# A decoder layer in split float32: one weight sum of each seven-product step made by an accumulating transfer, and seven such steps of eight in the late chunks

## The chip, the cores and the metric

The kernel runs on one core of a Trainium2 chip. The metric is the device time of one execution in microseconds (us), the median of the runs; lower is better. The engines that matter here are TensorE (PE in the profile), VectorE (DVE), ScalarE (ACT), GpSimd (POOL) and SyncE (SP), which issues nearly all the loads. The transfers themselves run on 16 DMA engines that all the queues share.

## The reference

One layer over 256 tokens of 2048 features. Two gated feed-forward blocks stand around a mixer; the change touches only the first product of the feed-forward blocks.

```python
D_MODEL = 2048; SEQ = 256; D_FF = 5632

def swiglu(h, w_in, w_out):
    gu = h @ w_in                                  # (256, 2048) @ (2048, 11264)
    gate, up = gu[..., :D_FF], gu[..., D_FF:]
    return (jax.nn.silu(gate) * up) @ w_out        # (256, 5632) @ (5632, 2048)

h = h + 0.5 * swiglu(rmsnorm(h, ffn1_norm), ffn1_w_in, ffn1_w_out)
...                                                # pooling mixer and gated linear attention
h = h + 0.5 * swiglu(rmsnorm(h, ffn2_norm), ffn2_w_in, ffn2_w_out)
out = rmsnorm(h, final_norm)
```

All inputs and outputs are float32.

## The kernel before

**Split products.** A float32 number is held as a high part (a cast to the type fp32r, made by ACT, `L155`) and a low part (the number minus its high part, made by DVE, `L156`). A product of two such blocks is three matmuls: high by high, high by low, low by high (`three`, matmuls at `L191`). Every weight block that PE uses has to be split first, since weights are read from memory once each.

**Steps.** Weights come in steps of four blocks of 128 x 512, two loads of 512 KB each (`load`, `L135`): two blocks of input rows by two blocks of output columns, B11, B12, B21 and B22. Against the two token tiles (128 tokens each) such a step is a 2 by 2 block product. It is done in one of two ways. An *S step* makes all eight block products: 24 matmuls, and DVE makes four low parts (2048 columns). A *W step* is one step of a Strassen-Winograd scheme: seven block products, 21 matmuls, for which DVE also makes four differences of weight blocks (`less`, `L179`) and then the low parts of seven blocks in all. The activations' sums S1 to S4 that the scheme needs are made once for each pair of input blocks that may be used so (`W_PAIRS`, `s_make`). `KINDS` says which steps of a chunk are W and which are S.

**Chunks.** The 5632 hidden columns are 11 chunks of 512. `first_product(c)` multiplies chunk c of gate and up in eight steps, then gates and transposes the result. `second_product` multiplies finished chunks by the output weights, in S steps only; from chunk 2 on a first product of eight steps alternates with a second product over two chunks, four S steps. So a period in the middle of a feed-forward block has 12 steps. The first feed-forward block has names with f (`ps_fi`, `pw_fi`, `ps_fo`), the second with z.

**The combine.** The W steps of a chunk add four of their products up in the two tiles `pw_..._0` and `pw_..._1` of the accumulator memory. When the last W step is through, `combine` reads them: ACT copies one half of `pw_0` (`L297`), DVE makes four sums (`L298` to `L301`; the first reads the other half of `pw_0`, and `L301` is the last to read `pw_1`). The next second product accumulates in the space of the same two tiles: its token tile 0 takes that of `pw_0`, tile 1 that of `pw_1`. Then `L483` adds the sums to the chunk's own accumulators, `L490` and `L492` gate them, and `L505` splits the transposed result.

**Buffers.** Raw weights land in four slots of four blocks (three named `ring_raw`, one more `fring_raw` or `zring_raw`, taken in rotation). Split blocks go to a ring of 22 block places (16 named `ring_hi`, `ring_lo`, 6 more `fring_...` or `zring_...`); a block's place is free once PE has used it. A run of blocks that meets the end of either part of the ring is split in two by `parts_of`.

**Order.** Every engine works its queue in order. The order of each queue is fixed at build time by a scheduler that models how long the instructions take; the program's text gives only the dependences. SP issues a load as soon as the blocks of the slot that it overwrites have been read for the last time.

**POOL** issues the accumulating stores of half sums (`hd<-half`, `L537`: 512 KB added to a tensor in memory), two after each second product but the last ones, and does little else.

Of the kernel before, what the change touches and what calls it, by code (L numbers as in the profile page):

```python
# [33 lines left out]
ALU = mybir.AluOpType  # L34
PSUM = bass.MemoryType.PSUM

P = 128
# [5 lines left out]
CW = 512  # L43
# [15 lines left out]

W_PAIRS = (1, 3, 4, 6, 2, 5)  # L60
CHUNKS = ("WWWWWWSS",) * 8
KINDS = {
# [11 lines left out]
MORE_RAW = 1  # L74
MORE_RING = 6
WIDE = True
# [6 lines left out]
def layer(ctx: ExitStack, tc: tile.TileContext, io):  # L83
    nc = tc.nc
# [82 lines left out]
    def s_step(src, parts=1, runs=WIDE):  # L167

        w = load(src, parts=max(parts, 2)).rearrange("p (b c) -> p b c", c=CW)
        b = parts_of(w, SINGLES if parts == 4 else PAIRS if parts == 2 or not WIDE else ALL)  # L170
        return lambda k, n: b[n if k == 0 else 3 - n]

    def w_step(src):

        w = load(src).rearrange("p (b c) -> p b c", c=CW)
        f = dict(zip(("B11", "B22", "B21"), parts_of(w, (slice(0, 1), slice(2, 4)))))

        def less(out, x, y):
            nc.vector.tensor_tensor(out=out, in0=x, in1=y, op=ALU.subtract)  # L179


        less(w[:, 0:2, :], w[:, 1:2, :].broadcast_to([P, 2, CW]), w[:, 0:4:2, :])
        less(w[:, 2, :], w[:, 2, :], w[:, 0, :])
        less(w[:, 3, :], w[:, 3, :], w[:, 2, :])
        f.update(zip(("T1", "T3", "T2", "T4"), parts_of(w, PAIRS)))
        return f

    def three(ps, a, b, start, stop, **kw):

        for i, (x, y) in enumerate(((a[0], b[0]), (a[0], b[1]), (a[1], b[0]))):  # L190
            nc.tensor.matmul(ps, x, y, start=start and i == 0, stop=stop and i == 2, **kw)  # L191

    class Group:
# [66 lines left out]
        def w(self, a, s, b):  # L260

            if self.one is None:
# [6 lines left out]
                first = True  # L269
# [8 lines left out]
            three(p16[:, 0, :], a(0, 0), b["B11"], first, last)  # L278
            three(p75[:, 1, :], s["S1"], b["T1"], first, last)
            three(p75[:, 0, :], s["S3"], b["T3"], first, last)  # L280
# [7 lines left out]
        def combine(self):  # L288
# [6 lines left out]
            c, d = self.add  # L295
            u2 = d[:, 1, :]
            nc.scalar.copy(out=c[:, 0, :], in_=p16[:, 0, :])  # L297
            nc.vector.tensor_tensor(out=u2, in0=p16[:, 1, :], in1=c[:, 0, :], op=ALU.add)  # L298
            nc.vector.tensor_tensor(out=c[:, 1, :], in0=p75[:, 1, :], in1=u2, op=ALU.add)
            nc.vector.tensor_tensor(out=d[:, 0, :], in0=p75[:, 0, :], in1=u2, op=ALU.add)  # L300
            nc.vector.tensor_tensor(out=d[:, 1, :], in0=p75[:, 1, :], in1=d[:, 0, :], op=ALU.add)  # L301

# [831 lines left out]
```

## Time and profile before

| | |
|---|---|
| median of three runs | 1702.04 us (1701.92 to 1702.26) |
| span of the profiled execution | 1702.4 us, so 0.36 us above the median |
| PE, PEld, DVE, ACT, POOL busy | 1689.7, 1403.1, 1411.5, 999.3, 62.9 us |
| transfers | 365.30 MB, 215 GB/s over the span |
| a period of first and second product, first feed-forward block | 62.14 us, DVE busy in 59.10 us of it |

A matmul of 512 columns is listed with about 390 ns, but matmuls overlap: they start 0.227 us apart where PE has its operands. The same holds on DVE, where a listed duration is some 0.09 us longer than the distance of starts. What an instruction costs its engine is read from the distance of starts.

### The profile page before, as it was taken

To read this page: it belongs to the slowest core of one execution; us is meant where nothing else is said; L and a number is where in the kernel's file an instruction comes from. 1 tells how busy PE (TensorE), PEld (TensorE's weight loads), DVE (VectorE), ACT (ScalarE), POOL (GpSimd) and SP (SyncE) were. 2 spreads that over 40 slices of the span, in tenths; PEclk is the share of its full clock that TensorE was granted. 3 is DMA by queue.
4 is the path that set the end of the run, shared out by engine and by line. 5 is a ranking of instruction groups with operands and counts; after the bars stand their busy time and mean duration, and the time that the engine had idled before them with its cause. 6 is when DMAs were issued, how large, how long until landed. Compare 5 with 4: busy or idle time off the path is not lost.

```text
span 1702.4 us, 20984 instructions
## 1 busy us (share of the span) xinstructions
PE 1689.7 (99%) x7705; PEld 1403.1 (82%) x7705; DVE 1411.5 (83%) x1565; ACT 999.3 (59%) x1272; POOL 62.9 (4%) x70
## 2 busy tenths in 40 slices
PE   9999999999999999999999999999999999999997
PEld 7888888888888888888988888888888888888886
DVE  8779999999999996645564677999999999998974
ACT  7655666665666664563454554666656656566553
POOL 0000000000000000000000000000000000000012
PEclk9999999999999999999999999999999999999999
DMA  9856856857767776554665764676666667677781
GB/s 355 338 142 229 259 156 229 269 165 221 259 178 221 246 240 215 185 182 139 197 214 169 228 203 155 196 249 195 214 244 208 203 235 227 192 245 218 215 298 50
DMA packets 105241, 365.30 MB, mean 215 GB/s; under 512 B 11809, under 2 KB 15009, under 8 KB 105138
## 3 DMA queue, kind: packets, MB, share of 16 engines
q1 hardware_dynamic: 97026, 335.63, 58.1%
q0 software_dynamic: 7392, 27.27, 8.1%
q8 instruction: 60, 0.98, 0.2%
q10 hardware_dynamic: 720, 1.07, 0.2%
q14 instruction: 43, 0.35, 0.1%
HBM read 338.75 MB, written 25.17 MB: 214 GB/s over the span
## 4 chain that ended last, share of the span: by engine, by line
PE 91%; DVE 5%; DMA 2%; issue 1%; ACT 1%; SPq 0%; POOL 0%; POOLq 0%; ACTq 0%; DVEq 0%
PE ps_fi L191 17%; PE ps_zi L191 14%; PE ps_fo L191 14%; PE ps_zo L191 12%; PE pw_fi L191 8%; PE pw_zi L191 7%; PE ps_h L191 5%; PE ps_mp L191 3%; PE ps_mv L191 3%; DVE ring_lo L156 2%; PE ps_mg L191 2%; PE ps_mq L191 1%; DMA ring_raw<-in_ffn_w_out 1%; PE ps_w_mk L191 1%; DVE ring_raw L179 1%
## 5 line engine op out<-in xcount | busy, mean ns | idle before, releaser
L155 ACT CAST ring_hi<-ring_raw 128x1024 fp32r<-128x1024 f32 (+3 forms) x544 | 501.4, 942 | 381.6 <-DMA ring_raw<-in_ffn_w_in 79.8
L156 DVE TENSOR_TENSOR ring_lo<-ring_raw,ring_hi 128x1024 fp32r<-128x1024 f32 (+6 forms) x463 | 573.8, 1250 | 182.5 <-ACT ring_hi L155 181.4
L179 DVE TENSOR_TENSOR ring_raw<-ring_raw 128x512 f32<-128x512 f32 (+1 forms) x243 | 207.4, 862 | 0.3
L155 ACT CAST zring_hi<-ring_raw 128x1024 fp32r<-128x1024 f32 (+1 forms) x113 | 99.6, 887 | 54.5 <-DMA ring_raw<-in_ffn_w_out 11.8
L191 PE MATMUL ps_fi<-ring_lo,xT_hi 128*128 128x512 f32 x324 | 126.5, 390 | 0.5 <-DVE ring_lo L156 0.4
L191 PE MATMUL ps_fi<-ring_hi,xT_lo 128*128 128x512 f32 x324 | 125.8, 389 | 0.0
L191 PE MATMUL ps_fi<-ring_hi,xT_hi 128*128 128x512 f32 x324 | 124.2, 390 | 1.2 <-ACT ring_hi L155 1.2
L156 DVE TENSOR_TENSOR zring_lo<-ring_raw,zring_hi 128x1024 fp32r<-128x1024 f32 (+3 forms) x101 | 112.2, 1117 | 11.9 <-ACT zring_hi L155 11.8
L155 ACT CAST ring_hi<-zring_raw 128x1024 fp32r<-128x1024 f32 (+1 forms) x85 | 84.2, 991 | 48.0 <-PE ps_zi L191 22.8
L191 PE MATMUL ps_zi<-ring_lo,h_hi 128*128 128x512 f32 x288 | 112.1, 389 | 0.0
L191 PE MATMUL ps_zi<-ring_hi,h_lo 128*128 128x512 f32 x288 | 112.1, 390 | 0.0
L191 PE MATMUL ps_zi<-ring_hi,h_hi 128*128 128x512 f32 x288 | 111.3, 390 | 0.0
L156 DVE TENSOR_TENSOR ring_lo<-zring_raw,ring_hi 128x1024 fp32r<-128x1024 f32 (+2 forms) x65 | 94.2, 1451 | 7.4 <-ACT ring_hi L155 7.3
L191 PE MATMUL ps_fo<-ring_lo,fhi 128*128 128x512 f32 x240 | 93.9, 391 | 0.0
L191 PE MATMUL ps_fo<-ring_hi,flo 128*128 128x512 f32 x240 | 93.8, 391 | 0.0
L191 PE MATMUL ps_fo<-ring_hi,fhi 128*128 128x512 f32 x240 | 93.4, 391 | 0.0
L191 PE MATMUL pw_zi<-ring_hi,s_z 128*128 128x512 f32 x262 | 92.5, 389 | 0.0
L191 PE MATMUL ps_zo<-ring_lo,zhi 128*128 128x512 f32 x234 | 91.5, 391 | 0.0
L191 PE MATMUL ps_zo<-ring_hi,zlo 128*128 128x512 f32 x234 | 91.4, 391 | 0.0
L191 PE MATMUL ps_zo<-ring_hi,zhi 128*128 128x512 f32 x234 | 90.7, 390 | 0.0
L191 PE MATMUL pw_fi<-ring_hi,s_f 128*128 128x512 f32 x226 | 78.7, 389 | 0.0
L155 ACT CAST ring_hi<-fring_raw 128x512 fp32r<-128x512 f32 (+1 forms) x69 | 56.9, 832 | 33.6 <-DVE fring_raw L179 9.8
(324 smaller groups left out, 3730.5 us busy)
## 6 DMA issues: line engine op xcount, KB each, us to landing
ring_raw<-in_ffn_w_in SPq DMA_DIRECT2D x262, 512.0 KB, 5.6
ring_raw<-in_ffn_w_out SPq DMA_DIRECT2D x136, 512.0 KB, 5.2
fring_raw<-in_ffn_w_in SPq DMA_DIRECT2D x44, 512.0 KB, 5.5
zring_raw<-in_ffn_w_in SPq DMA_DIRECT2D x44, 512.0 KB, 4.3
ring_raw<-in_w_out_mix SPq DMA_DIRECT2D x32, 512.0 KB, 4.3
fring_raw<-in_ffn_w_out SPq DMA_DIRECT2D x20, 512.0 KB, 6.0
zring_raw<-in_ffn_w_out SPq DMA_DIRECT2D x20, 512.0 KB, 6.0
hd<-half_f POOLq DMA_DIRECT2D x18, 512.0 KB, 8.1
```

What stands on the lines that cost most here:

```text
L155: nc.scalar.copy(out=hi[:, j:k, :], in_=src[:, i + j : i + k, :])
L156: nc.vector.tensor_tensor(out=lo, in0=src[:, i : i + n, :], in1=hi.bitcast(F32), op=ALU.subtract)
L179: nc.vector.tensor_tensor(out=out, in0=x, in1=y, op=ALU.subtract)
L191: nc.tensor.matmul(ps, x, y, start=start and i == 0, stop=stop and i == 2, **kw)
```

## The change

Block order and signs of the W step are chosen anew, so that one of the four sums that it needs, Q1 = B12 + B11, can be made where B12 lies: after the load, a transfer issued by POOL reads B11 once more from memory (256 KB) and adds it to the block. DVE then makes three differences in two instructions instead of four in three: first one block, Q1 - B22, then in one instruction of two blocks B11 and B21 minus that. The low parts are made in two instructions, of three blocks (B11, B22, B21) and of four (Q1, T3, T2, T4), where they were four instructions of one and two blocks. In the combine two sums become differences. The late chunks (3 to 10) of both feed-forward blocks have seven W steps and one S step instead of six and two; for this the activation sums of one more pair are made, and the ring has 21 places instead of 22.

```diff
-W_PAIRS = (1, 3, 4, 6, 2, 5)
-CHUNKS = ("WWWWWWSS",) * 8
+W_PAIRS = (1, 3, 4, 6, 2, 5, 0)
+CHUNKS = ("WWWWWWWS",) * 8
...
-MORE_RING = 6
+MORE_RING = 5
...
     def w_step(src):
         w = load(src).rearrange("p (b c) -> p b c", c=CW)
-        f = dict(zip(("B11", "B22", "B21"), parts_of(w, (slice(0, 1), slice(2, 4)))))
+        nc.gpsimd.dma_start(out=w[:, 0, :], in_=src[:, CW : 2 * CW], accum_op=ALU.add)
+        f = dict(zip(("B11", "B22", "B21"), parts_of(w, (slice(1, 4),))))
...
-        less(w[:, 0:2, :], w[:, 1:2, :].broadcast_to([P, 2, CW]), w[:, 0:4:2, :])
-        less(w[:, 2, :], w[:, 2, :], w[:, 0, :])
-        less(w[:, 3, :], w[:, 3, :], w[:, 2, :])
-        f.update(zip(("T1", "T3", "T2", "T4"), parts_of(w, PAIRS)))
+        less(w[:, 2, :], w[:, 0, :], w[:, 2, :])
+        less(w[:, 1:4:2, :], w[:, 1:4:2, :], w[:, 2:3, :].broadcast_to([P, 2, CW]))
+        f.update(zip(("Q1", "T3", "T2", "T4"), parts_of(w, ALL)))
...
-            three(p75[:, 1, :], s["S1"], b["T1"], first, last)
+            three(p75[:, 1, :], s["S1"], b["Q1"], first, last)
...
-            nc.vector.tensor_tensor(out=c[:, 1, :], in0=p75[:, 1, :], in1=u2, op=ALU.add)
+            nc.vector.tensor_tensor(out=c[:, 1, :], in0=p75[:, 1, :], in1=u2, op=ALU.subtract)
...
-            nc.vector.tensor_tensor(out=d[:, 1, :], in0=p75[:, 1, :], in1=d[:, 0, :], op=ALU.add)
+            nc.vector.tensor_tensor(out=d[:, 1, :], in0=p75[:, 1, :], in1=d[:, 0, :], op=ALU.subtract)
```

After the change the lines from `w_step` on have numbers lower by one (the combine is `L296` to `L300`). PE has 48 matmuls fewer and DVE 226 instructions fewer; POOL issues 126 transfers more.

DVE in the middle of the W steps of chunk 7, first feed-forward block, before: `L156` rows are low parts, `L179` rows differences.

```order
L156 TENSOR_TENSOR fring_lo<-fring_raw,fring_hi 128x512
L156 TENSOR_TENSOR ring_lo<-ring_raw,ring_hi 128x1024
L156 TENSOR_TENSOR fring_lo<-fring_raw,fring_hi 128x1024
L179 TENSOR_TENSOR ring_raw<-ring_raw 128x512
L179 TENSOR_TENSOR fring_raw<-fring_raw 128x1024
L156 TENSOR_TENSOR ring_lo<-ring_raw,ring_hi 128x1024
L179 TENSOR_TENSOR ring_raw<-ring_raw 128x512
L156 TENSOR_TENSOR ring_lo<-ring_raw,ring_hi 128x2048
```

The same place now, with the semaphores waited on (`DMAHW` are loads from SP, `DMASW` transfers from POOL):

```order
L156 TENSOR_TENSOR ring_lo<-ring_raw,ring_hi 128x1536 [waits DMAHW2_49,DMAHW1_49,Activation_49]
L180 TENSOR_TENSOR ring_raw<-ring_raw 128x512 [waits DMASW1_49,DVE_49]
L156 TENSOR_TENSOR ring_lo<-fring_raw,ring_hi 128x2048 [waits Activation_49]
L180 TENSOR_TENSOR ring_raw<-ring_raw 128x2x512 [waits DVE_49]
L156 TENSOR_TENSOR ring_lo<-ring_raw,ring_hi 128x1536 [waits DMAHW4_49,DMAHW3_49,Activation_49]
```

A W step is now a row of 1536, one of 512, one of 2 x 512 and one of 2048 columns (with further cuts at the ring's ends), and the row of 512 is where DVE waits for the accumulating transfer; between it and the row of 2 x 512 of the same step stands the last low part of the step before.

PE at the end of the W steps of chunk 6, second feed-forward block, before: the last products into `pw_zi6_0`, then rows of the chunk's own accumulator. The last W product and an S step follow, 27 starts from the last row of `pw_zi6_0` to the first of the second product, `ps_zo0_4_0`.

```order
L191 MATMUL ps_zi6_0_9516<-ring_hi_74,h2_lo3_6517 128x512
L191 MATMUL pw_zi6_0_9531<-ring_lo_75,s_z2_7271 128x512 [waits DVE_49]
L191 MATMUL pw_zi6_0_9531<-ring_hi_74,s_z2_7271 128x512
L191 MATMUL ps_zi6_1_9517<-ring_lo_75,h2_hi2_6512 128x512
L191 MATMUL ps_zi6_1_9517<-ring_hi_74,h2_lo2_6516 128x512
```

The same place now:

```order
L190 MATMUL pw_zi6_1_9389<-ring_hi_74,s_z3_7174 128x512
L190 MATMUL pw_zi6_0_9388<-ring_lo_75,s_z3_7174 128x512
L190 MATMUL pw_zi6_0_9388<-ring_hi_74,s_z3_7174 128x512
L190 MATMUL ps_zi6_1_9375<-ring_lo_75,h2_hi0_6414 128x512
L190 MATMUL ps_zi6_1_9375<-ring_hi_74,h2_lo0_6418 128x512
```

From the last row of `pw_zi6_0` to the first of `ps_zo0_4_0` there are now 15 starts; half of the one S step that is left stands ahead of the last W products. So it is in 14 of the 19 chunks that have W steps; in the other five it is 20 to 38. Before it was 27 to 45 in all.

POOL in the first feed-forward block now; before, its queue held only the `hd<-half` rows there:

```order
L176 DMA ring_raw<-in_ffn_w_in 128x512 [waits DMAHW3_49,DMASW0_49,DVE_49]
L176 DMA ring_raw<-in_ffn_w_in 128x512 [waits DMAHW5_49,DMASW5_49,DVE_49]
L536 DMA hd<-half_f_2128 128x1024 [waits DMASW2_49,Activation_49]
L536 DMA hd<-half_f_2131 128x1024 [waits Activation_49]
L176 DMA fring_raw<-in_ffn_w_in 128x512 [waits DMAHW7_49,DMASW6_49,DVE_49]
L176 DMA ring_raw<-in_ffn_w_in 128x512 [waits DMAHW1_49,DMASW7_49,DVE_49]
```

The accumulating transfers of the W steps (`L176`) and the half sums (`L536`) share POOL's one queue in order: here the last two of a chunk's seven stand behind the half sums of the second product that came before the chunk.

More of the change, by code (lines that the diff above doesn't have):

```diff
@@ L1082, in steps @@
         b = b.transpose(3, 0, 2, 1, 4, 5)
-        b = np.stack([b[:, :, :, 0, 0], b[:, :, :, 0, 1], b[:, :, :, 1, 1], b[:, :, :, 1, 0]], 3)
+        b = np.stack([b[:, :, :, 0, 1], b[:, :, :, 0, 0], b[:, :, :, 1, 1], b[:, :, :, 1, 0]], 3)
         return b.reshape(b.shape[0], b.shape[1], P, 4 * CW)
```

2 lines of the change are left out of this document (1 added, 1 removed).

## The prediction

> **What bounds the kernel now.** I read the page first, for the span and the busy engines.
>
> ```profile
> span 1702.4 us, 20984 instructions
> ...
> PE 1689.7 (99%) x7705; PEld 1403.1 (82%) x7705; DVE 1411.5 (83%) x1565; ACT 999.3 (59%) x1272; POOL 62.9 (4%) x70
> ...
> DVE  8779999999999996645564677999999999998974
> ...
> DMA  9856856857767776554665764676666667677781
> ```
>
> PE is busy for 99% of the span, but DVE is at 9 tenths or more through both feed-forward blocks, where the change acts. So the next views are the windows (one period of 12 steps, then the first chunk of the second block) and PE's waits.
>
> ```profile
> core 0: us, PE busy (x) PEld busy (x) DVE busy (x) ACT busy (x) POOL busy (x), PEclk, DMA share, GB/s
> ...
> 334.25:396.39 62.14, 62.14 (x280) 51.46 (x279) 59.10 (x63) 39.20 (x47) 1.73 (x2) 1.00 0.70 217
> ...
> 1001.16:1087.35 86.19, 86.19 (x389) 71.42 (x389) 71.64 (x103) 48.10 (x66) 2.76 (x2) 1.00 0.52 174
> ```
>
> ```profile
> PE idle L575 <- DVE zeros L570: 1.2, 1, 1.2
> PE ps_fi L191 <- ACT ring_hi L155: 1.2, 2, 0.8
> PE ps_fi L191 <- DVE ring_lo L156: 0.4, 2, 0.2
> ```
>
> PE waits 2.8 us in the whole execution. DVE has 62.14 - 59.10 = 3.0 us to spare in a period, and PE never pays for it. So PE bounds and DVE follows closely: a matmul less is time less, until DVE or a transfer comes too late.
>
> What a matmul costs is read from the chain, since the busy list counts overlapped ends:
>
> ```profile
> 272.11 10.88 PE ps_fo L191 x48
> ```
>
> 10.88 / 48 = 0.2267 us. A W step of 21 is then 4.76 us on PE, an S step of 24 is 5.44 us.
>
> DVE's costs are read from the distance of starts in its timeline, at the end of chunk 6:
>
> ```profile
> 380.01 1.22 DVE L156 TENSOR_TENSOR ring_lo<-ring_raw,ring_hi 128x1024 fp32r<-128x1024 f32 x1
> 381.15 0.69 DVE L179 TENSOR_TENSOR fring_raw<-fring_raw 128x512 f32<-128x512 f32 x1
> 381.75 0.69 DVE L156 TENSOR_TENSOR fring_lo<-fring_raw,fring_hi 128x512 fp32r<-128x512 f32 x1
> 382.35 2.29 DVE L156 TENSOR_TENSOR ring_lo<-ring_raw,ring_hi 128x2048 fp32r<-128x2048 f32 x1
> 384.56 0.69 DVE L156 TENSOR_TENSOR ring_lo<-fring_raw,ring_hi 128x512 fp32r<-128x512 f32 x1
> 386.68 2.29 DVE L156 TENSOR_TENSOR fring_lo<-ring_raw,fring_hi 128x2048 fp32r<-128x2048 f32 x1 [1.44 <-ACT fring_hi L155]
> 388.89 2.29 DVE L156 TENSOR_TENSOR ring_lo<-ring_raw,ring_hi 128x2048 fp32r<-128x2048 f32 x1
> 391.09 0.69 DVE L298 TENSOR_TENSOR add_fi<-pw_fi,add_fi 128x512 f32<-128x512 f32 x1
> ...
> 393.49 1.75 DVE L156 TENSOR_TENSOR ring_lo<-fring_raw,ring_hi 128x1536 fp32r<-128x1536 f32 x1
> 395.15 0.69 DVE L156 TENSOR_TENSOR fring_lo<-fring_raw,fring_hi 128x512 fp32r<-128x512 f32 x1
> 395.76 1.23 DVE L483 TENSOR_TENSOR ps_fi<-ps_fi,add_fi 128x1024 f32<-128x1024 f32 x1
> 396.89 0.68 DVE L301 TENSOR_TENSOR add_fi<-pw_fi,add_fi 128x512 f32<-128x512 f32 x1
> ```
>
> 512 columns take 0.60 us, 1024 1.14, 1536 1.66, 2048 2.21.
>
> **The change, part by part.** *PE.* Two blocks times eight chunks lose one S step for a W step: 16 x 3 = 48 matmuls, the very number of the row above, 10.88 us. All of it lies on the path.
>
> *DVE.* A W step now costs 0.60 + 1.14 for the first low parts, 1.14 + 2 x 0.60 for the differences, 2 x 1.14 for the last low parts: 6.36 us. Then it costs 1.66 + 0.60 + 1.14 + 2.21 = 5.61 us. The rest of a period is four sums (2.40), two `L483` (2.28) and four rows of 512 (2.40): 7.1 us. Before: 6 x 6.36 + 6 x 2.21 + 7.1 = 58.5, beside the 59.10 listed. After: 7 x 5.61 + 5 x 2.21 + 7.1 = 57.4 in a period of 62.14 - 0.68 = 61.46. DVE's spare time grows from 3.0 to about 4.1 us, so its sum doesn't bound. Nor do the steps lag more: in the W run DVE loses 6 x (6.36 - 4.76) = 9.6 us on PE before, 7 x 0.85 = 6.0 after. ACT casts the same columns in a W step and 1536 more for each S step turned into one, beside 22 us of idle time in the period. The activation sums of the seventh pair (some 2 us of DVE in each block) fall in the first chunk, where DVE idles 14 us of 86.19 while PE is full. The ring's lost place is one block of 21, three matmuls or 0.7 us of lead, less than the 3.6 us by which the W run's lag shrinks. These four I cost at nothing.
>
> *The accumulating transfer: its issue and load on the queues.* Rows of the half sums and of the queues:
>
> ```profile
> L537 POOL DMA_DIRECT2D hd<-half_f x18: 853/862/1006, 107.7 to 607.5; - x18
> ...
> DMA to landing us min/median/max: 5.5/8.1/11.3
> ```
>
> ```profile
> q1 hardware_dynamic: 97026, 335.63, 58.1%
> q0 software_dynamic: 7392, 27.27, 8.1%
> ...
> ring_raw<-in_ffn_w_in SPq DMA_DIRECT2D x262, 512.0 KB, 5.6
> ...
> out<-zh SPq DMA_DIRECT2D x4, 256.0 KB, 2.9
> ```
>
> 126 issues of 0.86 us are 108 us of POOL, which is busy 4%. A packet of q1 takes 0.581 x 1702.4 x 16 / 97026 = 0.163 us, one of q0, 4 KB for nearly all, 0.298. The new packets are 2 KB, 128 to a step: between 0.149 (half the bytes) and 0.298 each, so 1.2 to 2.4 us of the 16 engines in a W step, beside 256 x 0.163 / 16 = 2.6 for its load. I take the lower end, since load packets too cost by their bytes: 3.8 us, under PE's 4.76. The period's DMA share goes from 0.70 to (43.5 + 8.3) / 61.46 = 0.84.
>
> *Its latency.* No row shows 256 KB added to on-chip memory. The nearest is the row above, 512 KB added in memory: 5.5 to 11.3 us to landing. Half the bytes under the same loads end near its lower end; I take 5.5, and the range keeps 2.9 (the nearest transfer of 256 KB, the output store) and 11.3. Where is it late? SP loads a slot as soon as DVE is done with it, and within the W run 11 to 18 us of other DVE rows stand between that and the difference that needs the sum. The tight place is the first W step of a chunk:
>
> ```profile
> 273.33 0.62 ACT L155 CAST ring_hi<-ring_raw 128x512 fp32r<-128x512 f32 x1 [4.24 <-DMA ring_raw<-in_ffn_w_in]
> 278.62 1.22 DVE L179 TENSOR_TENSOR ring_raw<-ring_raw 128x1024 f32<-128x1024 f32 x1
> ```
>
> ACT waits for that load until 273.33, and DVE's first difference starts 5.3 us later, filled with other work. A transfer of 5.5 us ends 0.2 us after this; DVE's additional 1.1 us of spare time covers that: nothing. If it lands at x us, PE loses about x - 5.3 - 1.1 in each chunk. What waits behind it on DVE is the whole queue, low parts of the next steps included; on POOL the half sums, which nothing needs for tens of us.
>
> *The combine's cover.* Between the last W product into `pw_0` and the second product that takes its place PE has 15 starts now in 14 chunks, 3.40 us, where 27 (6.12 us) to 45 stood. In that time ACT must copy and DVE make the first sum. Before, at the place of the DVE rows above and at one in the second block:
>
> ```profile
> 387.39 0.39 PE L191 MATMUL pw_fi<-fring_hi,s_f 128*128 128x512 f32 x1
> 388.45 0.58 ACT L297 COPY add_fi<-pw_fi 128x512 f32<-128x512 f32 x1
> 396.23 0.39 PE L191 MATMUL ps_fo<-ring_hi,fhi 128*128 128x512 f32 x1
> 1443.70 0.45 PE pw_zi L191 x2
> 1446.63 0.68 DVE L298 TENSOR_TENSOR add_zi<-pw_zi,add_zi 128x512 f32<-128x512 f32 x1
> ```
>
> The sum is done 391.09 + 0.69 - 387.39 = 4.4 us after the last product, and 3.4 to 3.6 in the second block, with wide low parts ahead of it in DVE's queue and 8.8 us of cover at the first of the two places. With 3.40 us, PE would wait 1.0 and 0.1 us if DVE kept its place. The new order puts less ahead of the sum (on average 3.2 us of rows behind the last low part of the W run, 4.5 before), which takes most of it away; the wait that is left is scatter. The bounds are 0 and 14 x 1.0; I take 0.2 us a chunk, 3 us in all, near the lower end, since a row of 4.4 less 1.3 is under 3.40. The other reads of `pw` have 9.5 us or more.
>
> *The sum.* 1702.4 - 10.9 + 3 = 1694.5 for the profiled execution; this stands 0.36 above the median of the runs, so 1694.2.
>
> **Two rules of the Trainium skill.** The issue row says 853 to 1006 ns while DVE was over 90% busy. The Trainium skill's SBUF — State Buffer (SBUF: two separate sides) warns that a transfer issued from GpSimd gets no descriptors while DVE holds the shared port in a two-port mode, and says that `tensor_tensor`, the only kind in these rows, has no such mode; the trace agrees so far, as no issue took 0.2 us above the others. As a rival: an issue held up by one DVE row of 2.29 us lands at 5.5 + 2.3 = 7.8, and PE loses 1.4 us in 16 chunks, 22 less 10.9, so 1713. The landing row is 5.5 to 11.3 us for 512 KB. The Trainium skill's DMA: Bandwidth & Descriptors (Anatomy of one DMA — SWDGE (gpsimd) path) gives 2.0 us plus the bytes at 436 GB/s: estimates by that page are 3.2 us for 512 KB, which the trace does not show, and 2.6 us for 256 KB, by which the first W step would have 2.7 us to spare and the sum would be the same.
>
> **The rivals.** (1) *The transfer lands late at the first W step of a chunk.* It decides from a landing of 5.3 + 1.1 + 0.68 = 7.1 us: from there PE loses more than it saves. For it: the half sums' median is 8.1 us, and ACT already waits there. Against: half the bytes. At 8.1 us PE loses 1.7 us in 16 chunks: 1702.0 - 10.9 + 27 = 1718. (2) *The short combine eats the gain.* If DVE keeps the place of the first-block row, 14 x 1.0 us is lost, with the five other chunks unhurt: 1702.0 - 10.9 + 14 = 1705; with half of that 1698. For it: the 4.4 us. Against: the 3.4 to 3.6. (3) *DMA engines become the bound of the W run.* At 0.298 us for a 2 KB packet a W step needs 2.6 + 2.4 = 5.0 us, over PE's 4.76, and the half sums' 512 packets (9.5 us) come in the same run: 7 x 5.0 + 9.5 = 44.5 us of transfers while PE needs 33.3. Three steps of lead in the ring (14.3 us) cover the 11.2 between them only if the ring is full at the start. A loss of 1 to 2 us a chunk gives 1707 to 1723. (4) *Everything new is hidden.* 1702.0 - 10.9 = 1691.1. PE has 2.8 us of waits in all, so not much less than this can come.
>
> **How the numbers follow.** The forecast with its neighbours, 1692.5 to 1697: 0.42. Rival 4, to 1692.5: 0.18. Rival 2, 1697 to 1706: 0.17, of which a third under 1698.6. Rival 1: 0.13. Rival 3: 0.07. The held-up issue: 0.03. A measurement of this kernel tells 0.2%, 3.4 us, from no change. Faster by more: 0.42 + 0.18 + 0.05 = 0.65. Within it, 1698.6 to 1705.4: 0.11 of rival 2 and 0.02 of the lower ends of rivals 1 and 3: 0.13. Slower: 0.22. The range goes from 1690.5 to 1709, which leaves out the upper parts of rivals 1 and 3, 0.16 or so, and little below. The forecast's own range is 1691 to 1698.
>
> **What the profile would show.** 1: the second product's first step starts 61.5 us after the one before, where it was 62.14. 2: DVE rows of a W step in four, 1.66, 0.60, 1.14, 2.21 apart, some 57 to 58 us busy in a period. 3: the accumulating transfers' landing at a median near 5.5 us, and DVE's waits (`L180`, or `L156` at the ring's end) for transfers small. 4: PE's waits for the first sum of the combine at or below 3 us in total. The prediction is wrong if the landing is over 7 us, if PE waits for `L297` by a us or more in a chunk, or if loads take clearly over their present 5.6 us.

## The result, and the profile after

The changed kernel takes 1787.13 us (median of five runs, 1784.43 to 1791.99) against 1702.04 (1701.49 to 1703.94) for the kernel before in the same comparison: a ratio of 1.0497, 95% interval 1.0484 to 1.051. It is 5% slower, 85 us, and far outside the predicted range. The profiled execution took 1785.36 us, with a span of 1783.6. (Of `plain`, among the experiments, one of two runs was in the chip's slower state and is left out.)

The page after, in the order of the lines shown of before (span, busy engines, the queues in packets, MB and share of 16 engines), and from the list of transfers the rows of loads and of the new accumulating ones (the number at the end is the median from issue to landing):

```profile
PE 1716.4 (96%) x7657; PEld 1404.6 (79%) x7657; DVE 1395.2 (78%) x1303; ACT 1011.5 (57%) x1276; POOL 175.8 (10%) x196
...
q1 hardware_dynamic: 97026, 335.63, 55.3%
q0 software_dynamic: 25536, 60.30, 18.9%
...
ring_raw<-in_ffn_w_in SPq DMA_DIRECT2D x262, 512.0 KB, 6.2
...
ring_raw<-in_ffn_w_in POOLq DMA_DIRECT2D x97, 256.0 KB, 5.0
fring_raw<-in_ffn_w_in SPq DMA_DIRECT2D x44, 512.0 KB, 7.7
```

PE has its 48 matmuls less (7705 to 7657), and DVE has less work too (1411.5 to 1395.2 us). By share PE, DVE and ACT are all less busy than before; only POOL, which issues the new transfers, does more (4% to 10%). PE's idle time, span less busy, goes from 12.7 to 67.2 us. So the time went into waiting. PE's waits, where before had three rows of 2.8 us together (columns: total us, times, longest us; the line numbers after the change are one lower, `L297` to `L300` are the sums of the combine, `L190` the matmuls):

```profile
PE pw_fi L190 <- DVE ring_lo L156: 12.7, 9, 2.7
PE pw_zi L190 <- DVE ring_lo L156: 7.9, 7, 2.0
PE ps_zo L190 <- DVE add_zi L297: 6.3, 3, 2.9
PE pw_fi L190 <- ACT ring_hi L155: 5.7, 7, 1.6
PE pw_zi L190 <- ACT ring_hi L155: 5.6, 7, 1.8
PE ps_fo L190 <- DVE add_fi L297: 4.6, 2, 2.4
PE ps_zo L190 <- DVE ring_lo L156: 3.5, 2, 2.7
```

Over all rows PE waits 41.9 us for split blocks (1.6 before), 13.2 us for the combine (0 before) and 1.2 us at the start. The second loss is the clock:

```profile
core 0: 1783.6 us, clock 0.984
```

It was 0.998. A mean clock of 0.984 over 1783.6 us is 28.5 us of full speed not granted, 3.4 before: up to 25 us. The spans then compare as -10.9 (matmuls) + 53.5 (waits) + 25 (clock) = 67.6 of the 81.2 us by which the two profiled executions differ (the medians differ by 85.1). The other 13.6 I can't assign row by row; some 8 of them are the way a wait is counted, from the modelled end of the matmul ahead, 0.39 us after its start, though starts come 0.23 apart (49 waits x 0.16).

Where it happens: the windows of one period in the first block, from a second product's start to the next, and slices of 4 us at the end of the W run (columns as in the prediction: length, then PE, PEld, DVE, ACT and POOL busy, PEclk, DMA share, GB/s):

```profile
481.21:553.20 71.99, 66.20 (x277) 52.28 (x276) 60.89 (x49) 40.81 (x48) 9.26 (x11) 0.95 0.85 243
...
536.00:540.00 4.00, 3.90 (x17) 2.88 (x16) 4.00 (x3) 1.42 (x2) 0.00 (x0) 1.00 0.73 222
540.00:544.00 4.00, 1.86 (x6) 0.67 (x4) 3.83 (x3) 3.37 (x4) 0.00 (x0) 1.00 0.92 280
544.00:548.00 4.00, 2.19 (x5) 1.81 (x6) 2.36 (x2) 0.19 (x1) 0.86 (x1) 0.54 0.96 343
548.00:552.00 4.00, 4.00 (x12) 3.10 (x12) 2.08 (x2) 2.67 (x4) 0.86 (x1) 0.60 1.03 338
552.00:556.00 4.00, 4.00 (x19) 3.30 (x19) 3.66 (x5) 3.00 (x3) 0.00 (x0) 1.00 1.06 270
```

The period takes 71.99 us, where 62.14 stood (the eight periods of the block have a mean of 66.8). DVE is busy 60.89 of it, so it has 11 us to spare, and PE still waits: in the slices from 540 to 548 us PE runs 11 matmuls where some 35 fit. Then the column PEclk falls to 0.54 and 0.60. In the timeline these are the last matmuls of the W run (start, us, row, what ended the wait):

```profile
542.23 0.51 PE L190 MATMUL pw_fi<-ring_hi,s_f 128*128 128x512 f32 x1 [1.61 <-ACT ring_hi L155]
543.18 0.50 PE L190 MATMUL pw_fi<-ring_hi,s_f 128*128 128x512 f32 x1 [0.44 <-ACT ring_hi L155]
...
545.81 0.80 PE L190 MATMUL pw_fi<-ring_lo,s_f 128*128 128x512 f32 x1 [1.90 <-DVE ring_lo L156]
```

One delay behind these waits lies 20 us earlier, at a late load. POOL and DVE in the same period:

```profile
504.83 0.88 POOL L536 DMA_DIRECT2D hd<-half_f  x1 [0.98 <-ACT half_f L533]
506.19 0.89 POOL L536 DMA_DIRECT2D hd<-half_f  x1 [0.48 <-ACT half_f L533]
514.23 0.89 POOL L176 DMA_DIRECT2D fring_raw<-in_ffn_w_in  x1 [7.15 <-DMA fring_raw<-in_ffn_w_in]
...
519.46 1.76 DVE L156 TENSOR_TENSOR ring_lo<-ring_raw,ring_hi 128x1536 fp32r<-128x1536 f32 x1 [4.59 <-ACT ring_hi L155]
```

SP issued that load at 505.43, between the two stores of half sums; its second half landed 11.9 us after its issue, ACT's queue stood on it for 7.13 us, and DVE had nothing to do for 4.59 us. From 519.46 to 541.09 DVE then works without a pause, so the delay is carried on. A second one lies just ahead of PE's waits, in the queues of ACT and DVE:

```profile
540.18 1.05 ACT L155 CAST ring_hi<-fring_raw 128x1024 fp32r<-128x1024 f32 x1 [1.57 <-DMA fring_raw<-in_ffn_w_out]
541.14 1.99 ACT L155 CAST ring_hi<-ring_raw 128x1024 fp32r<-128x1024 f32 x2
...
541.26 2.29 DVE L156 TENSOR_TENSOR ring_lo<-fring_raw,ring_hi 128x2048 fp32r<-128x2048 f32 x1 [0.17 <-ACT ring_hi L155]
543.47 2.29 DVE L156 TENSOR_TENSOR ring_lo<-ring_raw,ring_hi 128x2048 fp32r<-128x2048 f32 x1
```

The rows of `fring_raw` are for the second product's weights. ACT stands 1.57 us on that load before it makes the casts of the last W step (541.14), for which PE waits first; DVE makes the load's wide low part before the one (543.47) for which PE waits 1.90 us. How much of PE's waits each delay makes isn't separated.

### The profile page after: what moved, and what is told of

Its sections match the earlier page's. It is cut to its first block, busy times and chain, and to the rows that moved or that the text cites. A ratio compares the mean times of both kernels' runs of the same rounds, so it can differ in the third digit from the quotient of the medians.

```text
span 1783.6 us, 21094 instructions
## 1 busy us (share of the span) xinstructions
PE 1716.4 (96%) x7657; PEld 1404.6 (79%) x7657; DVE 1395.2 (78%) x1303; ACT 1011.5 (57%) x1276; POOL 175.8 (10%) x196
## 3 DMA queue, kind: packets, MB, share of 16 engines
q0 software_dynamic: 25536, 60.30, 18.9%
## 5 line engine op out<-in xcount | busy, mean ns | idle before, releaser
L156 DVE TENSOR_TENSOR ring_lo<-ring_raw,ring_hi 128x2048 fp32r<-128x2048 f32 (+5 forms) x373 | 606.7, 1637 | 217.4 <-ACT ring_hi L155 216.9
L155 ACT CAST ring_hi<-ring_raw 128x1024 fp32r<-128x1024 f32 (+2 forms) x583 | 539.6, 954 | 386.4 <-DMA ring_raw<-in_ffn_w_in 61.4
L180 DVE TENSOR_TENSOR ring_raw<-ring_raw 128x512 f32<-128x512 f32 (+1 forms) x194 | 184.0, 953 | 3.6 <-DMA ring_raw<-in_ffn_w_in 2.4
L176 POOL DMA_DIRECT2D ring_raw<-in_ffn_w_in x97 | 84.0, 866 | 907.3 <-DMA ring_raw<-in_ffn_w_in 480.4
L190 PE MATMUL pw_zi<-ring_hi,s_z 128*128 128x512 f32 x298 | 109.1, 404 | 5.8 <-ACT ring_hi L155 5.6
L190 PE MATMUL ps_fo<-ring_hi,fhi 128*128 128x512 f32 x276 | 109.2, 396 | 2.8 <-DVE add_fi L297 2.4
L190 PE MATMUL ps_fo<-ring_lo,fhi 128*128 128x512 f32 x276 | 108.4, 393 | 0.0
L190 PE MATMUL ps_fo<-ring_hi,flo 128*128 128x512 f32 x276 | 108.3, 392 | 0.0
L190 PE MATMUL pw_fi<-ring_hi,s_f 128*128 128x512 f32 x278 | 102.0, 406 | 5.9 <-ACT ring_hi L155 5.7
L190 PE MATMUL ps_zo<-ring_hi,zhi 128*128 128x512 f32 x260 | 102.2, 394 | 4.8 <-DVE add_zi L297 3.4
L190 PE MATMUL ps_zo<-ring_lo,zhi 128*128 128x512 f32 x260 | 102.5, 394 | 3.5 <-DVE ring_lo L156 3.5
L190 PE MATMUL ps_fi<-ring_lo,xT_hi 128*128 128x512 f32 x259 | 102.5, 396 | 0.4 <-DVE ring_lo L156 0.2
L156 DVE TENSOR_TENSOR zring_lo<-ring_raw,zring_hi 128x1536 fp32r<-128x1536 f32 (+3 forms) x54 | 77.9, 1446 | 31.6 <-ACT zring_hi L155 31.5
L190 PE MATMUL ps_zo<-ring_hi,zlo 128*128 128x512 f32 x260 | 102.0, 392 | 0.0
L155 ACT CAST ring_hi<-fring_raw 128x1024 fp32r<-128x1024 f32 (+1 forms) x75 | 69.9, 952 | 56.6 <-DMA fring_raw<-in_ffn_w_in 20.8
L190 PE MATMUL ps_fi<-ring_hi,xT_lo 128*128 128x512 f32 x259 | 101.9, 394 | 0.0
L190 PE MATMUL ps_zi<-ring_lo,h_hi 128*128 128x512 f32 x250 | 98.7, 395 | 2.1 <-DVE ring_lo L156 2.0
L190 PE MATMUL ps_fi<-ring_hi,xT_hi 128*128 128x512 f32 x259 | 98.9, 391 | 1.2 <-ACT ring_hi L155 1.2
L190 PE MATMUL ps_zi<-ring_hi,h_hi 128*128 128x512 f32 x250 | 96.8, 394 | 1.4 <-ACT ring_hi L155 1.4
L190 PE MATMUL ps_zi<-ring_hi,h_lo 128*128 128x512 f32 x250 | 97.6, 392 | 0.0
L155 ACT CAST zring_hi<-ring_raw 128x1024 fp32r<-128x1024 f32 (+1 forms) x81 | 70.2, 885 | 41.6 <-DMA ring_raw<-in_ffn_w_in 24.9
```

Of the source, the lines that this page charges most:

```text
L155: nc.scalar.copy(out=hi[:, j:k, :], in_=src[:, i + j : i + k, :])
L156: nc.vector.tensor_tensor(out=lo, in0=src[:, i : i + n, :], in1=hi.bitcast(F32), op=ALU.subtract)
L176: nc.gpsimd.dma_start(out=w[:, 0, :], in_=src[:, CW : 2 * CW], accum_op=ALU.add)
```

## The experiments

All runs are against the kernel before on the same chip (1703.2 to 1705.7 us as the median of each group). The theories, numbered as the expectations name them: (1) the DMA engines' time, that is the added bytes; (2) the second transfer on a raw slot, behind its load, which holds the slot some 5 us longer; (3) the seventh W step, with one S step behind it; (5) the wide low parts; (6) the round trip of the raw slots; there is no (4). The scheduler orders each kernel's queues anew, so no edit moves only what it names; differences under some 10 us between two versions are not read as effects. The results together (PE's idle time is span less busy; waits are those of the profiled execution, for the combine and for split blocks, other waits not listed):

| kernel | us | ratio to before | PE idle | combine | blocks | clock |
|---|---|---|---|---|---|---|
| before | 1702.0 | 1 | 12.7 | 0 | 1.6 | 0.998 |
| after | 1787.1 | 1.0497 | 67.2 | 13.2 | 41.9 | 0.984 |
| `plain` | 1766.2 | one run | 58.5 | 11.5 | 35.8 | 0.989 |
| `halfplain` | 1768.7 | 1.038 | 58.6 | 10.7 | 37.0 | 0.985 |
| `tiny` | 1761.2 | 1.0336 | 54.0 | 16.1 | 26.6 | 0.991 |
| `nosum` | 1754.9 | 1.0293 | 52.9 | 15.5 | 26.4 | 0.989 |
| `dvesum` | 1820.1 | 1.0675 | 94.6 | 15.5 | 67.1 | 0.984 |
| `seven` | 1819.6 | 1.0673 | 96.0 | 23.7 | 60.9 | 0.990 |
| `six` | 1714.8 | 1.0071 | 20.9 | 2.3 | 6.6 | 0.998 |
| `dvesum6` | 1759.9 | 1.0323 | 48.0 | 4.3 | 31.9 | 0.993 |
| `beforewide` | 1712.2 | 1.0052 | 17.5 | 2.6 | 3.1 | 0.998 |
| `narrow7` | 1742.8 | 1.0246 | 46.8 | 4.0 | 31.2 | 0.991 |
| `narrow6` | 1722.7 | 1.0113 | 25.7 | 6.3 | 1.5 | 0.997 |
| `narrow6sum` | 1735.4 | 1.0189 | 33.0 | 1.4 | 20.4 | 0.996 |
| `raw5` | 1799.6 | 1.056 | 76.1 | 3.5 | 61.3 | 0.984 |
| `narrow7raw5` | 1763.1 | 1.0358 | 57.0 | 11.0 | 34.9 | 0.993 |
| `beforeraw5` | 1703.9 | 1.0002 | 13.7 | 0 | 2.3 | 0.998 |
| `sixraw5` | 1717.5 | 1.0086 | 22.0 | 0 | 9.7 | 0.997 |
| `sixfront` | 1755.5 | 1.0288 | 45.8 | 18.7 | 15.6 | 0.990 |
| `sixspread` | 1808.9 | 1.0621 | 88.0 | 73.8 | 2.0 | 0.979 |

**The bytes of the new transfer.** Three kernels take DMA work away and keep the seven W steps. `plain` overwrites the block instead of adding to it:

```diff
-        nc.gpsimd.dma_start(out=w[:, 0, :], in_=src[:, CW : 2 * CW], accum_op=ALU.add)
+        nc.gpsimd.dma_start(out=w[:, 0, :], in_=src[:, CW : 2 * CW])
```

> The changed kernel with the transfer of the W step as a plain write of the same 256 KB instead of an addition (the weight sum is not made); the order of every engine is the same as in the changed kernel (1787 us). Theory 1, transfer time: in the W run the accumulating packets (178 ns for 2 KB) and the half sums (328 ns for 4 KB) fill the 16 DMA engines, so the loads of the last W steps land late. A plain 2 KB packet took 84 to 90 ns before, so some 0.75 us of transfer time a W step, 5 us a period, goes: 1745 or less. Theory 2, slots: what counts is that the slot is held until a second transfer, issued only after the load, has landed (median 5.0 us), and that its next load starts so much later; bytes and packet times hardly matter: latency falls by under 1 us, 1770 or more. Theory 3, the seven W steps leave too little other work at the end of the run: no change, 1780 or more.

`halfplain` stores the half sums of the second product without adding them (`accum_op` left out of the store to `hd`):

> The changed kernel with the half sums stored plainly instead of added (the sums over earlier chunks are lost). 512 packets of 328 ns a period become 159 ns: 5.4 us less transfer time, all of it in the first half of the W run. Theory 1 (transfer time): 1750 or less. Theory 2 (slots held by the second transfer's latency): 1770 or more, since the W steps' own transfers are untouched. Theory 3 (too few S steps): 1780 or more.

`tiny` adds 8 of the 512 columns:

```diff
+        nc.gpsimd.dma_start(out=w[:, 0, :8], in_=src[:, CW : CW + 8], accum_op=ALU.add)
```

> The changed kernel with the W step's transfer cut to 8 of 512 columns (so the weight sum is made in 8 columns only): the second transfer and its place behind the load stay, its bytes go. Theory 1: DMA load as before the change, 1690 to 1710. Theory 2: the landing falls from 5.0 us to 2.5 to 3, so half of the loss at most comes back: 1735 to 1765. Theory 3: 1770 or more.

They took 1766.2 us (one run), 1768.7 (ratio 1.038, 1.0312 to 1.0447) and 1761.2 (1.0336, 1.0275 to 1.0397). Each gives back some 20 to 27 of the 85 us and none comes near 1702. `plain` and `halfplain` fall between the ranges of theories 1 and 2 and under that of theory 3, so no theory had them; `tiny` is in theory 2's range. Theory 1 falls as the whole cause, since with a transfer of almost no bytes 57 us stay, but 20 to 27 us go with the transfer time.

**The seventh W step, the rest of the change kept.**

```diff
-CHUNKS = ("WWWWWWWS",) * 8      # W_PAIRS with a seventh pair, MORE_RING = 5
+CHUNKS = ("WWWWWWSS",) * 8      # W_PAIRS of before, MORE_RING = 6
```

> The changed W step (accumulating transfer, wide low parts) with six W steps of eight and a ring of 22 as before the change. PE has the matmuls of the kernel before. Theory 1: a period has one accumulating transfer fewer and one S step more, the half sums still collide with the W run: 1715 to 1760. Theory 2: likewise, 1720 to 1770. Theory 3: the seventh W step is the cause, so 1700 to 1708.

`six` took 1714.8 us, ratio 1.0071 (1.0048 to 1.0094), just under the ranges of theories 1 and 2 and 7 us over theory 3's. Taking back the seventh W step, with its pair and its ring place, returns 72 us; the accumulating transfer and the wide low parts alone cost 11 us. PE's waits are then 11 us in all. The ring's place is not separated from the seventh step: every version with seven W steps has 21 places or fewer.

**With and without the second transfer.** `nosum` leaves the accumulating line of `plain` out, `dvesum` has a VectorE sum in its place, `dvesum6` is `dvesum` with six W steps, and `seven` is the kernel before with only the pattern of seven, its pair and the ring of 21 places.

```diff
-        nc.gpsimd.dma_start(out=w[:, 0, :], in_=src[:, CW : 2 * CW], accum_op=ALU.add)
...
+        nc.vector.tensor_tensor(out=w[:, 0, :], in0=w[:, 0, :], in1=w[:, 1, :], op=ALU.add)
         less(w[:, 2, :], w[:, 0, :], w[:, 2, :])
```

> The accumulating transfer of the W step is left out (the product P5 then uses B12 instead of B12+B11): no second transfer on a raw buffer at all, every instruction of VectorE, ScalarE and TensorE as in the changed kernel, seven W steps of eight. Theory 2 (the second transfer behind the load holds each of the four raw buffers some 5 us longer, so loads start too late): the loss goes, 1690 to 1710 us. Theory 3 (seven W steps in a row with one S step of cover for the combine cost the time, whatever the sum is made with): 1750 us or more, about what it was with the transfer of 8 of 512 columns. Theory 1 (the DMA engines' time) is no longer alone possible.

> The weight sum is made by a VectorE addition of 128x512 (0.60 us) in place of the accumulating transfer; seven W steps of eight. VectorE's work in a W step goes from 5.61 to about 6.2 us, 88 W steps. Theory 2 (second transfer holds the buffer): 1695 to 1720 us, since only the VectorE lag in the W run grows. Theory 3 (seven W in a row): 1760 us or more.

> The kernel before with seven W steps of eight and its own W step (four subtractions on VectorE, 6.36 us of it, low parts in two pieces), and a ring of 21: the seventh W step alone, with nothing else of the change. Theory 2 (second transfer holds the buffer): 1695 to 1725 us. Theory 3 (seven W in a row): 1765 us or more.

> Six W steps of eight, ring of 22, the new W step with its wide low parts, the sum on VectorE: the wide low parts and the other sign of one weight difference alone. VectorE's W step 6.36 to about 6.2 us. Theories 2 and 3 both: within 4 us of the kernel before (1704), since VectorE has time to spare; with the accumulating transfer this pattern took 1714.8, so theory 2 has the 11 us on the transfer and expects them gone here; theory 3 has nothing that says where the 11 us came from.

`nosum` took 1754.9 us (1.0293, 1.0257 to 1.033): without any second transfer, and with the same instructions on the other engines, 50 of the 85 us stay. So the transfer, its wait included, is worth some 33 us here. `tiny`, which keeps the second transfer and drops its bytes (its landing falls from 5.0 to 3.4 us), already gives back 26, so the wait for a transfer of any size, which is theory 2, has only some 6 us left, too little to be read. `seven` took 1819.6 (1.0673, 1.0635 to 1.071), 114 us more than the kernel before, and `dvesum` is as slow (1820.1). These two are no clean test of theory 3, since VectorE itself has more to do in them than TensorE: at the prediction's prices 7 x 6.36 + 5 x 2.21 + 7.1 = 62.7 us in a period of 61.46, and 61.6 in `dvesum`. `nosum` is cleaner, with the changed kernel's work on VectorE: it is in theory 3's range. So seven W steps are too many with wide low parts, whether or not a transfer makes the sum; what they cost with the low parts in pieces is shown below.

`dvesum6` missed what both theories gave it: 1759.9, though it has the pattern of before and no transfer. It differs from before in the wide low parts and in the order of the differences: of the last four operands, T3 and T4 come out of the last subtraction, so that no cast of a pair can start before all sums are made, where before T1 and T3 were ready after the first. The next four runs take that apart.

**The wide low parts.** `beforewide` changes only this in the kernel before; `narrow7`, `narrow6` and `narrow6sum` are after, `six` and `dvesum6` with the low parts in pieces.

```diff
-        f.update(zip(("T1", "T3", "T2", "T4"), parts_of(w, PAIRS)))   # before
+        f.update(zip(("T1", "T3", "T2", "T4"), parts_of(w, ALL)))     # beforewide
...
-        f = dict(zip(("B11", "B22", "B21"), parts_of(w, (slice(1, 4),))))               # after
-        f.update(zip(("Q1", "T3", "T2", "T4"), parts_of(w, ALL)))
+        f = dict(zip(("B11", "B22", "B21"), parts_of(w, (slice(1, 2), slice(2, 4)))))   # narrow7
+        f.update(zip(("Q1", "T3", "T2", "T4"), parts_of(w, PAIRS)))
```

> The kernel before with one edit: the last four operands of a W step (T1, T3, T2, T4) get their low parts in one VectorE operation of 128x2048 in place of two of 128x1024; everything else, six W steps of eight and the four subtractions on VectorE, as before. VectorE's rows say 2.21 us for the wide one against 2 x 1.14 us: 0.07 us less per step. Theory 5 (a wide operation can start only when both casts of ScalarE, 0.94 us each, and four places of the ring are there, so VectorE stands idle at it and the lows come too late in the W run): 1720 us or more. Theories 2 and 3 (the transfer, the seventh W step): within 4 us of 1704.

> The changed kernel, accumulating transfer and seven W steps of eight kept, with its low parts in the pieces of before (128x512 and 128x1024 for the first three operands, twice 128x1024 for the last four): about 0.15 us more VectorE work in a W step. Theory 5 (wide operations): at most 1740 us, if they carry most of the loss. Theory 3 (the seventh W step in a row): 1780 us or more, the added VectorE work makes it a little worse.

> Six W steps of eight, ring of 22, accumulating transfer, low parts in the pieces of before: the accumulating transfer alone. The same with wide low parts took 1714.8 us. Theory 5: the 11 us go, 1695 to 1705 us, since VectorE has some 0.6 us less to do in each W step than in the kernel before. Theory 2 (the second transfer holds the raw buffer): 1712 us or more.

> Six W steps of eight, ring of 22, the sum by a VectorE addition, low parts in the pieces of before; the same with wide low parts took 1759.9 us. VectorE's W step about 6.36 us, as in the kernel before. Theory 5: within 6 us of 1704. If it stays above 1740, it isn't the width of the low parts but the order in which the sums are made (the addition ahead of the other subtractions on VectorE).

`beforewide` took 1712.2 (1.0052, 1.0035 to 1.0069), 8.9 us more than before and not the 17 or more that theory 5 asked for. `narrow7` took 1742.8 (1.0246, 1.022 to 1.0271): 44 us less than after, half of the loss, with 0.15 us more DVE work per W step and with loads that take no less time (medians 6.6 and 8.2 us, where after has 6.2 and 7.7). It is 3 us over theory 5's range and far below theory 3's. But `narrow6` took 1722.7 (1.0113), 7 to 8 us more than the wide `six`, against theory 5, though too little to be read, and `narrow6sum` 1735.4 (1.0189), 25 less than `dvesum6` and still 32 above the kernel before, which has the same DVE work and the same pieces. So wide low parts cost time in two of the four pairs and make no readable difference in the other two, and the order of the differences, or what the scheduler makes of it, matters as well. As a single cause theory 5 falls, and so does theory 3: with pieces the seventh W step costs some 20 us (`narrow7` less `narrow6`), with wide low parts 72 (after less `six`). Most of the loss needs the two together.

**A fifth raw slot**, paid for with two places of the ring (`MORE_RAW = 1` to `2`, `MORE_RING` two less), in four kernels.

> The changed kernel with one more raw buffer in the late part (five in place of four, where each holds one load of 1 MB) and a ring of 19 places in place of 21 to pay for it. Theory 6 (the round trip load, accumulate, subtract, cast, low part, release of four raw buffers sets the pace of the W run): each buffer has a quarter more time for its trip, so the time falls by more than half of the loss, to 1705 to 1740 us. If the ring's places (how many operands may wait for TensorE) were the limit instead, two fewer make it worse: 1795 us or more.

> The changed kernel with the low parts in the pieces of before, five raw buffers and a ring of 19; the same with four buffers and 21 places took 1742.8 us. Theory 6 (round trip of the raw buffers): 1690 to 1715 us. Places of the ring as the limit: 1750 us or more.

> The kernel before with five raw buffers and a ring of 20 places in place of four and 22. TensorE is busy for 1689.7 of its 1702.4 us and waits for nothing there, so theory 6 has nothing to gain: 1700 to 1706 us, if 20 places are enough; more, if the ring's places already limit.

> Six W steps of eight with the accumulating transfer and wide low parts, five raw buffers and a ring of 20; with four and 22 it took 1714.8 us. Theory 6: the 11 us above the kernel before go, 1700 to 1706 us. Places of the ring as the limit: 1718 us or more.

1799.6 (1.056, 1.0542 to 1.0577), 1763.1 (1.0358), 1703.9 (1.0002, 0.9992 to 1.0012) and 1717.5 (1.0086). With seven W steps a slot more and two places less cost 12 to 20 us; with six they make no difference that can be read. So theory 6 falls as it was put, and for the loaded kernels two places of the ring are worth more than a slot. Slot and places changed together, so what a slot alone would do isn't shown.

**Where the S steps stand.** `six`, with the same six W and two S steps per chunk in another order:

```diff
-CHUNKS = ("WWWWWWSS",) * 8
+CHUNKS = ("SWWWWWWS",) * 8      # sixfront;  sixspread: "WWWSWWWS"
```

> The version with six W steps, accumulating transfer and wide low parts (WWWWWWSS, 1714.8 us), its late chunks in the order SWWWWWWS: the same steps, the run of six as long, but one S step (24 matmuls, 5.4 us) behind it in place of two. (a) the cover of the combine: 1740 to 1775 us, most of the 72 us between six and seven W steps. (b) the lag over the run: within 8 us of 1715, the run is as long as before. (c) the number of W steps: within 4 us of 1715.

> The same with the order WWWSWWWS: two runs of three, one S step between them, one behind the last. (a) the cover of the combine: 1740 to 1775 us, as with SWWWWWWS. (b) the lag over the run: 1705 to 1716 us, since VectorE and the loads catch up in the middle; if SWWWWWWS is slow and this is not, it is the lag at the end of a run that meets the short cover. (c) the number: within 4 us of 1715.

`sixfront` took 1755.5 us (1.0288, 1.0259 to 1.0317), some 40 more than `six`, and `sixspread` 1808.9 (1.0621, 1.0595 to 1.0646), 94 more. Neither the amount of work nor the length of the run explains that: the steps are the same, and the run is as long in the one and half as long in the other. (a), the cover of the combine, is the theory that holds for `sixfront`, with `sixspread` worse than it said. From the last product into `pw` to the second product there are 38 starts in most chunks of `six`, 15 in most of `sixfront` and 18 or 19 in most of `sixspread`. PE's waits name it, of `six`, `sixfront` and `sixspread` in this order:

```profile
PE ps_zo L190 <- DVE add_zi L300: 1.2, 1, 1.2
...
PE ps_zo L190 <- DVE add_zi L297: 1.1, 1, 1.1
```

```profile
PE ps_fo L190 <- DVE add_fi L297: 13.4, 4, 4.3
...
PE ps_zo L190 <- DVE add_zi L297: 4.0, 8, 0.9
```

```profile
PE ps_fo L190 <- DVE add_fi L297: 36.8, 7, 7.0
PE ps_zo L190 <- DVE add_zi L297: 35.7, 9, 5.8
```

In `sixspread` nearly every chunk pays, 72.5 us over 16 waits, and the clock falls to a mean of 0.979. One of these waits, in `sixspread`'s timeline: PE's last product into `pw`, ACT, DVE, PE's first matmul of the second product:

```profile
481.61 0.39 PE L190 MATMUL pw_fi<-ring_hi,s_f 128*128 128x512 f32 x1
...
484.18 1.05 ACT L155 CAST fring_hi<-ring_raw 128x1024 fp32r<-128x1024 f32 x1 [2.81 <-DMA ring_raw<-in_ffn_w_out]
...
487.55 0.58 ACT L296 COPY add_fi<-pw_fi 128x512 f32<-128x512 f32 x1
...
487.15 2.29 DVE L156 TENSOR_TENSOR fring_lo<-ring_raw,fring_hi 128x2048 fp32r<-128x2048 f32 x1 [4.27 <-ACT fring_hi L155]
489.37 1.75 DVE L156 TENSOR_TENSOR ring_lo<-ring_raw,ring_hi 128x1536 fp32r<-128x1536 f32 x1
491.03 0.68 DVE L297 TENSOR_TENSOR add_fi<-pw_fi,add_fi 128x512 f32<-128x512 f32 x1
...
491.77 0.79 PE L190 MATMUL ps_fo<-ring_hi,fhi 128*128 128x512 f32 x1 [5.69 <-DVE add_fi L297]
```

`pw` is complete at 482 us. But ACT's copy stands in its queue behind casts of the next loads, the first of which has no data until 484.18; the copy runs at 487.55, 5.9 us after the last product. DVE's first sum stands behind two wide low parts of the same loads and ends at 491.7, 10.1 us after it. With 38 matmuls of cover (8.6 us, as in `six`) PE would have waited 1.5 us; with the 19 of this place (4.3 us) it waits 5.8, of which the row lists 5.69. In `six` the same first sum ends 3.5 to 8.9 us after the last product, and PE waits 2.3 us for the combine in the whole execution: late there too, but covered. `sixspread` has more cover than `sixfront` and loses more; its first sum comes later, 5.8 to 10.7 us after the last product in its late chunks, where `sixfront` has 2.8 to 7.8. Why it is later there isn't shown.

## Why the prediction was wrong

**PE: right.** 48 matmuls are gone, 10.9 us.

**DVE's work: right, and its use was the error.** The timeline of after has the differences and low parts as priced (distances of starts 1.14 behind an `L180` of two blocks, 2.2 behind a wide low part):

```profile
535.47 2.28 DVE L156 TENSOR_TENSOR ring_lo<-ring_raw,ring_hi 128x2048 fp32r<-128x2048 f32 x1
537.67 1.22 DVE L180 TENSOR_TENSOR ring_raw<-ring_raw 128x1024 f32<-128x1024 f32 x1
538.81 2.28 DVE L156 TENSOR_TENSOR ring_lo<-ring_raw,ring_hi 128x2048 fp32r<-128x2048 f32 x1
```

From the sum of the rows the prediction went to "nor do the steps lag more" and cost four items at nothing, the lag of the W run and the ring's place among them. This is the step that failed, and it was sized wrong by the largest amount: PE waits 41.9 us for split blocks, where the prediction had none. DVE's spare time is no cover, since DVE works in a fixed order: in the period followed above it stands 4.59 us on the casts of a late load, and its 11 idle us go by unused. The wide low parts were counted as a gain of 0.15 us of DVE's time a step; `narrow7` shows that with seven W steps they cost 44 us. So work per period was right and told nothing of when a block is ready.

**The transfer's packets and latency: sized about right; that they cost nothing: wrong.** It was taken to land in 5.5 us; the medians are 5.0 us for the three slots `ring_raw` and 7.2 and 6.6 for the fourth. The rows of the fourth slot, beside the one above:

```profile
fring_raw<-in_ffn_w_in POOLq DMA_DIRECT2D x18, 256.0 KB, 7.2
...
zring_raw<-in_ffn_w_in POOLq DMA_DIRECT2D x11, 256.0 KB, 6.6
```

Its 2 KB packets take 0.176 us by the rows (18.9% of 16 x 1783.6 us, less 7392 packets of half sums at 0.298, over 18144), near the lower end taken, and the engines' share is 0.85 in the period, as predicted; but it is no even 0.85, with 0.96 to 1.06 in the slices from 544 to 556 us. The Trainium skill's estimate from DMA: Bandwidth & Descriptors (Anatomy of one DMA — SWDGE (gpsimd) path), 2.6 us, is half of what the trace shows under this load. The issues took 850 to 942 ns, so none was held up. But PE does not wait at the first W step of a chunk, as rival 1 had it: apart from the start its waits for blocks come from the fourth step of a chunk on, as at 540 to 548 us in the period above. "Within the W run 11 to 18 us of other DVE rows stand between": these rows are themselves behind the load and the transfer. `nosum` puts the transfer at some 33 us with seven W steps, where it was costed at nothing, and `tiny` puts most of that on its bytes, nearer to rival 3 than to rival 1.

**The combine: right mechanism, size wrong.** 3 us were taken, with 14 as the upper bound; PE waits 13.2. The working held the first sum's distance to the last product at what before shows, 3.4 to 4.4 us, and let it shrink. Those were two places: over the 19 chunks of before it ranges from 1.7 to 6.6 us, and in after from 1.7 to 6.9. The scatter was there already, and 15 starts of cover no longer hold it. The chain of waits shows sums behind a late load at one place in the second block, there the last sum, `L300`, which token tile 1 needs (what DVE does for a load issued at 1643.3 us stands ahead of the chunk's sums, and PE waits behind them):

```profile
1643.36 7.84 DMA ring_raw<-in_ffn_w_out
...
1652.00 0.69 DVE ring_lo L156
1652.69 1.14 DVE ps_zi L482
1653.83 0.60 DVE add_zi L300
1654.43 0.04 issue
1654.47 8.70 PE ps_zo L190 x37
```

And its price was set too low in kind: `sixfront` and `sixspread` lose 40 and 94 us with waits of 18.7 and 73.8 us for the combine. Part of it is clock that follows the waits (0.990 and 0.979), and in `sixfront` the waits for blocks grow too, from 6.6 to 15.6 us. How much of the 72 us of the seventh W step is the cover and how much the blocks' lag isn't separated for the changed kernel: its waits are three parts blocks to one part combine, while in `sixfront` half is combine.

**The clock was in no term.** 13 stretches of half clock, 51 us, lie inside the work of after, one of 3.4 us in before. Twelve of the 13 follow waits for operands; the last, in the mixer, is the one that before has too.

**Rivals.** The profile's signs were named rightly: loads over 5.6 us (6.2 and 7.7), PE waiting for `L297` by a us or more (five waits, up to 2.9). No rival reached 1787, since each was priced as if the others did not happen. At the places followed, late loads, late blocks, a late combine and a slower clock hang together, and taking out the transfer, the seventh W step or the wide low parts returns 33, 72 and 44 us, more than the whole loss in sum: the terms that were each held to be hidden don't simply add. That all of the loss is this one chain isn't shown.

What stays open: a kernel whose queues put the copy and the first sum ahead of the casts and low parts of loads still in flight, with seven W steps, would test the order itself. It wasn't tried, as the order comes from the scheduler. Nor is it shown why wide low parts cost 44 us with seven W steps and nothing readable with six and the transfer. No version ran faster than the kernel before; the only one level with it is the kernel before with a fifth raw slot.

## What to carry to other kernels

Idle time of an engine that works a fixed order is no cover: before you cost a term at nothing, look up what stands ahead of it in its queue, and whether that waits for a load. Price the slack between producer and consumer where it is shortest, here the 15 matmuls that were left behind the last product, not the mean over a period. When a change spends several slacks at once (a transfer behind a load, one cover step less, coarser pieces), price them together: here taking out one of three returned 33, 72 or 44 of the 85 us.

## What the hardware showed that was not expected

TensorE's clock falls to half after short waits. In the slices above PE waits 1.61, 0.44 and 1.90 us within 5.6 us and then runs at 0.54 and 0.60; elsewhere in after one wait for the combine of 2.2, 2.4 or 2.9 us was enough, while single waits of 2.3, 2.7 and 2.7 us were not followed by it. Matmuls then start 0.42 us apart in place of 0.23, for 3.4 or 6.8 us. The Trainium skill, TensorE: Matmul & The Clock Gate (HAM oscillation — how this bites in real kernels), gives as a rule that gaps over about 3.4 us are to be avoided; the length of the stretches agrees with its window, but here no single wait reached 3.4 us in after (the longest is 2.9), so several short ones, or one of 2.2 us, can do it too, and the length of one wait doesn't decide it.

A transfer added behind a load costs more than its own 1.4 us of engine time (128 packets of 0.176 us on 16 engines): the loads' median for the three slots `ring_raw` is 6.2 us with it, 5.2 without it (`nosum`) and 5.6 before, and one load beside two half sums took 11.9 us.
